# Two plain projections become seven-product pairs, and the scans are packed closer

## The chip, the cores and the metric

The kernel runs on one core of a Trainium2 chip. The metric is the device time of one execution in microseconds (us); the times below are medians over runs, and the profile is one execution taken by the hardware profiler. PE is the matrix engine (TensorE), PEld its weight loads, DVE the vector engine, ACT the scalar engine, POOL GpSimd, SP the engine that issues most DMAs. [...]

## The reference

One layer on 1024 tokens of width 1024, in fp32: two gated feed-forward blocks (width 2816) around a mixer, each behind an RMS norm.

```
h = h + 0.5 * swiglu_ffn(rmsnorm(h, ffn1_norm), ffn1_w_in, ffn1_w_out)
u = rmsnorm(h, mix_norm) @ w_mix_in
cb, cc, ch, gq, gk, gv, gz, gb, ga = split(u)        # 3 x 512, 4 x 512, 4, 4
y_conv = rmsnorm64(cb * causal_conv3(cc * ch)) * conv_out_norm
q, k, v = silu(causal_conv4([gq, gk, gv]))           # 4 heads of 128, q and k normed
beta = sigmoid(gb);  g = -exp(A_log) * softplus(ga + dt_bias)
o = gated_delta_rule_chunked(q, k, v, g, beta)       # a chain of states over chunks
y_gdn = rmsnorm(o, norm_w) * silu(gz)
h = h + concat([y_conv, y_gdn]) @ w_mix_out
h = h + 0.5 * swiglu_ffn(rmsnorm(h, ffn2_norm), ffn2_w_in, ffn2_w_out)
return rmsnorm(h, final_norm)
```

The delta rule solves a triangular system in each chunk and carries a state from chunk to chunk. `cc` is the c gate of the short convolution, `gz` the z gate of the delta rule's output.

## The kernel before, in words

**Products.** Every fp32 operand is split into a high and a low part (`split`, `wsplit`: a cast on ACT, L104, and a subtraction on DVE, L105), and every product is three matmuls (`mm3`, L196 to L200): high x high, low x high, high x low, each 128 x 128 weights against 128 x 512 moving data. Each `mm3` also calls `tick`, a count of groups by which small work is put off with `later(n, f)`.

**Pairs of seven products.** Two column tiles of a weight matrix, the two halves of the contraction and the two halves of the tokens make a 2 x 2 block product, done with seven products instead of eight (class `Pair`, L355 to L485). A product is four `mm3`. The activations' blocks and their sums (A11, A12, S1, nS2, S3, S4, A22) come from class `Blocks`; the weights' sums T1 to T4 are made for each pair on POOL (L112; DVE for the first pairs). `all_pairs` lists the tasks: two pairs run side by side, product by product (`twos`), and the first two products of later pairs (`head1`, `head2`) are put ahead of or between the products of earlier ones. `done` is called with each finished quarter C11, C12, C21, C22.

**Tasks.** A task has a load, a preparation and a run. `run_tasks` runs them in order, with preparations 4 tasks and loads 9 tasks ahead.

**Order.** The code emits instructions in this order; the planner of the framework then lays them on the engines' queues by priority and its own estimate of durations, so a ready `mm3` can be put ahead of a small operation that is not ready. Each engine and each DMA queue works its queue in order.

**Stages.** f1 (first feed-forward) ends near 640 us. The qkv stage (640 to 780 us) runs six pairs over `w_qkv`, in the order n = 4, 6, 0, 2, 8, 10; each finished column tile is stored with its halo (`u_dr`), and the first token half goes through the width-4 convolution (`conv4`, L951) at once, except for n = 10 and 11, whose first halves are stored to `v_dr` and convolved later. In the same stage `project_ba` makes the beta and decay inputs; `gates` (L910) then computes beta and g, in one call of some 30 small DVE operations.

The mixing stage (780 to 1166 us) has these parts:

- `rest`, a generator of plain projections. A unit (`unit_steps`, L1369) is one column tile, two token halves of eight `mm3` each; the generator yields after each `mm3`. There are four z units, then for each of four tiles a c, an h and a b unit: 16 units, 256 `mm3`. A c unit's result is kept in a tile `cc` (L1400), an h unit multiplies it in (L1409) and does the width-3 convolution, a b unit multiplies (L1420) and starts the group norm. `pump(n)` advances `rest` by n `mm3`.
- `late_convs`: 14 convolutions from `v_dr` and `u_dr`.
- `build(c)`, seven steps for each of eight chunks: decay, k k^T, q k^T and scaled copies, stored to DRAM.
- `solve(g)`: inverts 32 x 32 diagonal blocks of four chunks by rows on DVE (L1208, L1212), through DRAM (`diag_l`, `diag_x`).
- `finish(c)` (five steps) assembles a chunk's inverse out of 32- and 64-wide matmuls; `scan(c)` takes the chunk through the state: three links that alternate PE and DVE (L1282, L1287, L1298), the output (L1306, L1307), its norm (L1323, L1327), a transpose and the product with z (L1332), and the store to `y_dr` (L1334).
- `mix_out(part, hf)`: output projection of the convolution part (0) or the delta-rule part (1) for a token half, 32 `mm3` each.

Six chunks are built with 2.7 `mm3` of `rest` at each step (`PACE[0]`). Then scans run in a pipeline in which the next chunk begins after five steps of the last, with 2.05 `mm3` at each scan step and at each step of the last two builds (`PACE[1]`). `scan` forces all z units to be done before chunk 0's output. When chunk 3 is through, the remaining `rest` is emptied, and the order is `mix_out(1, 0)`, `mix_out(0, 0)`, `mix_out(0, 1)`, with two scan steps after each task, then all that is left of the scans, then `mix_out(1, 1)`. f2 (second feed-forward) follows in a new pool scope.

## Time and profile before

| | us |
|---|---|
| median of 3 runs | 1817.4 |
| lowest, highest | 1814.96, 1817.43 |
| profiled execution | 1817.63 |
| its span, first to last instruction | 1815.9 |

| engine | busy us | share |
|---|---|---|
| PE | 1784.8 | 98% |
| PEld | 1456.4 | 80% |
| DVE | 1350.4 | 74% |
| ACT | 738.7 | 41% |
| POOL | 545.5 | 30% |

The mean granted clock of PE is 0.996 of full speed. Busy time is the time in which at least one instruction of the engine was under way; matmuls overlap, so an interval in which PE is 100% busy can still hold more or fewer of them.

In a view of windows a row has the stretch, its length, then for PE, PEld, DVE, ACT and POOL the busy time and the count of instructions, then the granted clock, the DMA engines' share and GB/s. In a view of waits a row has the engine and line that waited, for what, and us in total, number, longest. In a timeline a row has the start, the duration, engine, line, operation, operands; in brackets the idle time before it and what ended it. In a group's row: count, total busy, mean ns of one, idle time before them.

### The profile page before, as it was taken

Reading aid. Unit: us, or ns where it says so; the run is one execution under the profiler, and the core shown is the slowest. Engines: PE = TensorE matmul, PEld = TensorE weight load, DVE = VectorE, ACT = ScalarE, POOL = GpSimd, SP = SyncE. Lnnn points to the kernel's source line nnn. Section 1 sums busy time; section 2 is a strip of 40 time slices with the busy share of each in tenths; the row PEclk is TensorE's granted clock in tenths of the full one; section 3 lists DMA queues with packets and bytes.
Section 4 is the critical chain, followed back from the end, with each engine's and each line's share of the span. In section 5 each row is a group of like instructions: output and inputs, shape, how many; then the busy total and the mean of one; then the engine's idle time right before and its main releaser. Section 6 shows DMA issues by size and latency. Waiting matters only on the chain.

```text
span 1815.9 us, 24900 instructions
## 1 busy us (share of the span) xinstructions
PE 1784.8 (98%) x8476; PEld 1456.4 (80%) x8476; DVE 1350.4 (74%) x2180; ACT 738.7 (41%) x1471; POOL 545.5 (30%) x382
## 2 busy tenths in 40 slices
PE   9999999999999999999999999999999999999997
PEld 6887778888888877778878887788888888888886
DVE  7898877677765889888867666897666666677675
ACT  7532222223534564468342334552222232344443
POOL 0000034446341411302210013016445544435153
PEclk9999999999999999999999999999999999999998
DMA  7435544336974543478854586524433434587542
GB/s 279 161 129 179 175 145 134 128 116 218 335 262 133 167 156 103 147 228 264 258 175 146 154 273 187 173 70 134 158 120 116 150 135 133 167 307 272 199 143 89
DMA packets 198352, 318.75 MB, mean 176 GB/s; under 512 B 28624, under 2 KB 49104, under 8 KB 198224
## 3 DMA queue, kind: packets, MB, share of 16 engines
q1 hardware_dynamic: 195200, 311.85, 51.7%
q10 hardware_dynamic: 3024, 5.30, 0.9%
q8 instruction: 67, 1.10, 0.3%
q14 instruction: 61, 0.50, 0.1%
HBM read 230.54 MB, written 86.53 MB: 175 GB/s over the span
## 4 chain that ended last, share of the span: by engine, by line
PE 43%; DMA 2%; DVE 2%; ACT 1%; issue 1%; POOL 1%; SPq 0%; ACTq 0%; POOLq 0%; DVEq 0%
PE ps_ps L197 12%; PE ps_ps L199 12%; PE ps_ps L198 12%; PE ps_mm L197 2%; PE ps_mm L198 2%; PE ps_mm L199 2%; DMA h<-h_dr 1%; PE ps_aux L1053 1%; DMA raw<-w_mo 1%; PE ps_aux L1079 0%; DVE xb L1212 0%; DVE sv L1208 0%; DVE wlo L105 0%; PE ps_aux L1307 0%; PE ps_aux L1059 0%
## 5 line engine op out<-in xcount | busy, mean ns | idle before, releaser
L197 PE MATMUL ps_ps<-hi,whi 128*128 128x512 f32 x1400 | 547.6, 392 | 5.3 <-DVE c L467 1.9
L199 PE MATMUL ps_ps<-hi,wlo 128*128 128x512 f32 x1400 | 544.8, 390 | 1.2 <-DVE wlo L105 1.1
L198 PE MATMUL ps_ps<-lo,whi 128*128 128x512 f32 x1400 | 545.2, 389 | 0.1
L197 PEld LDWEIGHTS ps_ps<-hi,whi 128*128 128x128 f32 x1400 | 262.8, 188 | 67.9 <-DVE c L467 5.3
L199 PEld LDWEIGHTS ps_ps<-hi,wlo 128*128 128x128 f32 x1400 | 262.8, 188 | 59.5 <-DVE wlo L105 4.9
L112 POOL TENSOR_TENSOR T<-raw 128x512 f32<-128x512 f32 x112 | 173.2, 1547 | 444.9 <-DMA raw<-w_in 230.0
L198 PEld LDWEIGHTS ps_ps<-lo,whi 128*128 128x128 f32 x1400 | 262.9, 188 | 54.5 <-DVE lo L733 0.5
L105 DVE TENSOR_TENSOR wlo<-raw,whi 128x512 fp32r<-128x512 f32 x280 | 239.7, 866 | 74.7 <-ACT whi L104 73.7
L105 DVE TENSOR_TENSOR wlo<-T,whi 128x512 fp32r<-128x512 f32 x244 | 214.4, 890 | 90.3 <-ACT whi L104 87.1
L199 PE MATMUL ps_ps<-ghi,wlo 128*128 128x512 f32 x616 | 241.1, 391 | 0.5 <-DVE wlo L105 0.4
L197 PE MATMUL ps_ps<-ghi,whi 128*128 128x512 f32 x616 | 241.1, 391 | 0.0
L198 PE MATMUL ps_ps<-glo,whi 128*128 128x512 f32 x616 | 240.6, 391 | 0.0
L104 ACT CAST whi<-T 128x512 fp32r<-128x512 f32 x244 | 146.5, 616 | 128.3 <-PE ps_ps L198 44.6
L104 ACT CAST whi<-raw 128x512 fp32r<-128x512 f32 x280 | 169.1, 617 | 60.4 <-DMA raw<-w_out 16.3
L197 PE MATMUL ps_mm<-hi,whi 128*128 128x512 f32 x384 | 157.2, 409 | 1.2 <-DVE u L478 1.2
L105 DVE TENSOR_TENSOR glo<-raw,ghi 128x512 fp32r<-128x512 f32 x154 | 125.0, 811 | 39.9 <-ACT ghi L104 39.2
L198 PE MATMUL ps_mm<-lo,whi 128*128 128x512 f32 x384 | 151.2, 394 | 0.0
L199 PE MATMUL ps_mm<-hi,wlo 128*128 128x512 f32 x384 | 150.8, 393 | 0.0
L199 PEld LDWEIGHTS ps_ps<-ghi,wlo 128*128 128x128 f32 x616 | 115.8, 188 | 26.8 <-DVE wlo L105 1.3
L198 PEld LDWEIGHTS ps_ps<-glo,whi 128*128 128x128 f32 x616 | 115.9, 188 | 25.6
L197 PEld LDWEIGHTS ps_ps<-ghi,whi 128*128 128x128 f32 x616 | 115.8, 188 | 25.3
L104 ACT CAST ghi<-raw 128x512 fp32r<-128x512 f32 x154 | 95.0, 617 | 65.6 <-DMA raw<-f2A 20.0
(254 smaller groups left out, 2144.7 us busy)
## 6 DMA issues: line engine op xcount, KB each, us to landing
raw<-w_in SPq DMA_DIRECT2D x264, 256.0 KB, 4.3
raw<-w_out SPq DMA_DIRECT2D x154, 256.0 KB, 4.2
raw<-w_qkv SPq DMA_DIRECT2D x36, 256.0 KB, 3.3
f1S<-S SPq DMA_DIRECT2D x33, 256.0 KB, 3.8
raw<-f1A SPq DMA_DIRECT2D x33, 256.0 KB, 3.7
raw<-f1S SPq DMA_DIRECT2D x33, 256.0 KB, 3.7
f2S<-S SPq DMA_DIRECT2D x33, 256.0 KB, 4.9
raw<-f2A SPq DMA_DIRECT2D x33, 256.0 KB, 4.4
```

The source lines that it names most:

```text
L104: tc.keep_in_program_order(nc.scalar.copy(out=hi, in_=src))
L105: nc.vector.tensor_tensor(out=lo, in0=src, in1=hi.bitcast(F32), op=ALU.subtract)
L112: tc.keep_in_program_order(nc.gpsimd.tensor_tensor(out=out, in0=in0, in1=in1, op=op))
L197: nc.tensor.matmul(out=ps, lhsT=whi, rhs=xhi, start=start, stop=False, skip_group_check=True)
L198: nc.tensor.matmul(out=ps, lhsT=whi, rhs=xlo, start=False, stop=False, skip_group_check=True)
L199: nc.tensor.matmul(out=ps, lhsT=wlo, rhs=xhi, start=False, stop=stop, skip_group_check=True)
L1053: nc.tensor.matmul(out=ps[:, sl], lhsT=lhs[:, sl], rhs=rhs[:, sl], start=start, stop=stop)
```

## The change

- `all_pairs` gets `heads_at`, which says behind which pair of pairs (`a`) the heads of which later pairs are put; the default is as before.
- The four c units leave `rest` and become two pairs (`c_pair`) at the end of the qkv stage, side by side (`twos` = 0, 2, 4, 6); their heads lie among the products of pairs 2 and 4. Their quarters are stored to `c_dr`, and an h unit loads its `cc` from there when each of its halves begins.
- The convolutions of n = 10 and 11 are done at once, as the others; `v_dr` goes, and `late_convs` has 12 entries.
- `gates` becomes a generator and runs one piece per tick.
- `rest` is now three z units, four times h and b, and the fourth z unit: 12 units, 192 `mm3`. `PACE[1]` is 1.38 instead of 2.05.
- `scan` no longer forces z: the z tile is loaded when `z_done`, and until then the last step is held (`HOLD`); `pipeline` lets the other chunks go on. The rings of `ot` and `zt` tiles get more buffers from rings that the builds used.
- The scan loop ends at `conv_done` instead of chunk 3. The last z unit's `mm3` are spread over six tasks, each followed by scan steps (`go_on`), so that the loads of the output projection, nine tasks ahead, are issued while they run.
- The output projection's order becomes (0, 0), (1, 0), (0, 1), (1, 1), with scan steps after each task. `mix_out(1, hf)` makes sure, when it is prepared, that its chunks are scanned, and loads `y` then.

```diff
-PACE = (2.7, 2.05)
+PACE = (2.7, 1.38)
+LATE_PACE = 1.8
...
-    def all_pairs(pairs, x, norm2, between={}, twos=(0, 2), n_early=EARLY, n_inside=INSIDE):
+    def all_pairs(pairs, x, norm2, between={}, twos=(0, 2), n_early=EARLY, n_inside=INSIDE, heads_at=None):
...
+        if heads_at is None:
+            heads_at = {0: soon}
...
                 if a > 0 or n > 1:
+                    soon = heads_at.get(a, ()) if n == 2 else ()
                     task(*two[0])
-                    for p in soon if a == 0 and n == 2 else ():
+                    for p in soon:
                         task(*p.head1())
                     task(*two[1])
-                    for p in soon if a == 0 and n == 2 else ():
+                    for p in soon:
                         task(*p.head2())
...
+        def by_ticks(steps):
+            if next(steps, steps) is not steps:
+                later(1, lambda: by_ticks(steps))
...
             if hf == 1:
-                gates()
+                by_ticks(gates())
...
             for n in (11, 9, 7, 5, 3, 1):
                 nc.vector.tensor_tensor(out=poly, in0=poly, in1=s2, op=ALU.mult)
                 nc.vector.tensor_scalar(out=poly, in0=poly, scalar1=1.0 / n, scalar2=None, op0=ALU.add)
+                yield
...
-        v_dr = [dram.tile([P, HALF + 3], F32, name=f"v_dr{n}") for n in range(HEADS)]
+        c_dr = [[dram.tile([P, HALF], F32, name=f"c_dr{t}{hf}") for hf in range(NH)] for t in range(4)]
...
-                    if n < 2 * HEADS + 2:
-                        conv4(n + i, 0, t1, temp(F32, "cv"))
-                    else:
-                        nc.sync.dma_start(out=v_dr[n + i - 2 * HEADS], in_=t1[:, 0:HALF + 3])
+                    conv4(n + i, 0, t1, temp(F32, "cv"))
...
-        pairs = [qkv_pair(n) for n in (4, 6, 0, 2, 8, 10)]
+        def c_pair(t):
+            def first(ps):
+                c = temp4(F32, "c11")
+                nc.scalar.copy(out=c[:, 3:HALF + 3], in_=ps)
+                return c
+
+            def done(name, tile_):
+                hf, i = int(name[1]) - 1, int(name[2]) - 1
+                nc.sync.dma_start(out=c_dr[t + i][hf], in_=tile_[:, 3:HALF + 3])
+
+            return Pair(xm, (w_cv[4 + t], w_cv[5 + t]), first, done)
+
+        pairs = [qkv_pair(n) for n in (4, 6, 0, 2, 8, 10)] + [c_pair(t) for t in (0, 2)]
         early_heads(pairs[:EARLY])
-        all_pairs(pairs, xm, nm[1], {0: lambda: project_ba(0), 2: lambda: project_ba(1)}, (0, 2, 4))
+        all_pairs(pairs, xm, nm[1], {0: lambda: project_ba(0), 2: lambda: project_ba(1)}, (0, 2, 4, 6),
+                  n_inside=1, heads_at={2: pairs[6:7], 4: pairs[7:8]})
 
-        order = [w_z[t] for t in range(HEADS)] + [w_cv[i * 4 + t] for t in range(4) for i in (1, 2, 0)]
+        order = [w_z[t] for t in range(3)] + [w_cv[i * 4 + t] for t in range(4) for i in (2, 0)] + [w_z[3]]
...
-            zt = gt_tile("zt", 1)
-            while not z_done:
-                next(rest)
-            nc.sync.dma_start(out=heads(zt), in_=z_dr[hf][:, :, ts])
-            ot = gt_tile("ot", 1)
+            def get_z():
+                zt = gt_tile("zt")
+                nc.sync.dma_start(out=heads(zt), in_=z_dr[hf][:, :, ts])
+                return zt
+
+            yt = get_z() if z_done else None
+            ot = gt_tile("ot")
...
             yield
+            while not z_done:
+                yield HOLD
+            yt = yt or get_z()
             yield
             pyt = flip(ot)
-            yt = zt
-            nc.vector.scalar_tensor_tensor(out=yt, in0=pyt, scalar=vcol(V_GN), in1=zt, op0=ALU.mult, op1=ALU.mult)
+            nc.vector.scalar_tensor_tensor(out=yt, in0=pyt, scalar=vcol(V_GN), in1=yt, op0=ALU.mult, op1=ALU.mult)
...
-                def evac_c(hf, ps):
+                def get_c(hf):
                     cc = mx.tile([P, HALF], F32, name="cc", tag="cs", bufs=3)
-                    nc.scalar.copy(out=cc, in_=ps)
+                    nc.sync.dma_start(out=cc, in_=c_dr[t][hf])
                     ccs.append(cc)
...
-                for evac in (evac_c, evac_h, evac_b):
-                    yield from unit_steps(evac)
+                yield from unit_steps(evac_h, get_c)
+                yield from unit_steps(evac_b)
 
         def others():
-            yield from z_steps()
+            yield from z_steps(range(3))
             yield from conv_steps()
+            conv_done.append(True)
+            yield from z_steps([3])
+            z_done.append(True)
...
-        while CPH - 1 not in scanned:
+        while not conv_done:
             next(scans)
             pump(PACE[1])
             next(side, None)
...
+                if u == 0 and part:
+                    while (hf + 1) * CPH - 1 not in scanned:
+                        advance()
+                    for f in (get, put):
+                        for k in range(4):
+                            f(k)
...
-        def between():
-            for _ in range(2):
-                next(scans, None)
-
-        n_first = len(tasks)
-        task(lambda: [None for _ in rest])
-        mix_out(1, 0, False)
-        run_tasks(n_first + 5, between)
-        mix_out(0, 0, True)
+        steps = [0.0]
+
+        def advance():
+            next(scans, None)
+            next(side, None)
+
+        def go_on(n):
+            steps[0] += n / (LATE_PACE if CPH - 1 in scanned else PACE[1])
+            while steps[0] >= 1:
+                steps[0] -= 1
+                advance()
+
+        def part_of_rest(n):
+            for _ in range(n):
+                next(rest, None)
+                go_on(1)
+
+        for n in (3, 3, 2, 3, 3):
+            task(lambda n=n: part_of_rest(n))
+        task(lambda: [go_on(1) for _ in rest])
+        n_rest = len(tasks)
+        mix_out(0, 0, False)
+        mix_out(1, 0, True)
         task(lambda: norms2[0].after(8, 4))
         norms2[0].then(lambda: [x2.norm1(norms2[0].rb, d) for d in range(KT)])
         mix_out(0, 1, False)
-        run_tasks(len(tasks), between)
-        for _ in scans:
-            pass
-        while queue:
-            tick()
         mix_out(1, 1, True, lambda u: [x2.split1(d) for d in (2 * u, 2 * u + 1)])
...
-        run_tasks(n_mix)
+        run_tasks(n_rest)
+        run_tasks(n_mix, lambda: go_on(4))
```

More of the change, by code (lines that the diff above doesn't have):

```diff
@@ L1364, in conv_norm, with unit_steps @@
             later((16, 10, 10, 7)[t], reduce)
-        z_done = []
-        def unit_steps(evac):
+        z_done, conv_done = [], []
+        def unit_steps(evac, begin=None):
             w = ahead.pop(0)
@@ L1373, in unit_steps @@
             for hf in range(NH):
+                if begin is not None:
+                    begin(hf)
                 ps = psum("mm")
@@ L1381, in unit_steps, with z_steps @@
                 yield
-        def z_steps():
-            for t in range(HEADS):
+        def z_steps(which):
+            for t in which:
                 def evac(hf, ps):
@@ L1391, in z_steps @@
                 yield from unit_steps(evac)
-            z_done.append(True)
         def conv_steps():
@@ L1457, in pipeline @@
                     live.append([gens.pop(0), 0])
+                moved = False
                 for e in list(live):
-                    if next(e[0], live) is live:
+                    said = next(e[0], live)
+                    if said is live:
                         live.remove(e)
-                    else:
+                    elif said is not HOLD:
                         e[1] += 1
+                        moved = True
                         yield
+                if live and not moved:
+                    yield
         scanned = set()
@@ L1521, in tile_hybrid, with mix_out, get, put @@
         norms2 = [Norm(h2[0], "mm"), Norm(h2[1])]
-        def mix_out(part, hf, last, also=None):
+        def mix_out(part, hf, last, also=None, then=None):
             bank = "mm"
-            ys, w = [], {}
+            ys, w = [None] * 4, {}
+            at_once = () if part else range(4 if hf else 3)
+            def get(k):
+                ys[k] = load(y_dr[part][hf][k // 2][:, k % 2, :])
+            def put(k):
+                ys[k] = split(ys[k], slot)
             def loads(u):
                 if u == 0:
-                    ys[:] = [load(y_dr[part][hf][k // 2][:, k % 2, :]) for k in range(4)]
+                    for k in at_once:
+                        get(k)
                 w[u] = [load(w_mo[part, u][:, i * HALF:(i + 1) * HALF]) for i in range(2)]
@@ L1533, in ready @@
                 if u == 0:
-                    ys[:] = [split(y, slot) for y in ys]
+                    for k in at_once:
+                        put(k)
                 w[u] = [wsplit(r) for r in w[u]]
@@ L1539, in ready, with ready_too @@
                         tc.keep_in_program_order(nc.scalar.dma_start(out=h2[hf][d], in_=h_dr[hf][d]))
+                if u == 0 and part:
[4 more added lines that the diff above has]
+                            f(k)
+            def ready_too(u):
+                if u == 0 and len(at_once) == 3:
+                    get(3)
+                    put(3)
+                if also is not None:
+                    also(u)
             def run(u, dd):
```

18 lines of the change are left out of this document (13 added, 5 removed).

## The prediction

> **What bounds the kernel now.** I read the page first (busy shares), then the windows, PE's waits, and the timeline where a wait stood.
>
> ```profile
> span 1815.9 us, 24900 instructions
> PE 1784.8 (98%) x8476; PEld 1456.4 (80%) x8476; DVE 1350.4 (74%) x2180; ACT 738.7 (41%) x1471; POOL 545.5 (30%) x382
> L197 PE MATMUL ps_mm<-hi,whi 128*128 128x512 f32 x384 | 157.2, 409 | 1.2 <-DVE u L478 1.2
> ```
>
> PE is busy 98%, so other engines matter only where they make it wait. The 409 ns of a matmul is its latency; its cost in a stream is the spacing of starts. These windows (us, then busy time and count of PE, weight loads, DVE, ACT, POOL, then the granted clock) give it:
>
> ```profile
> 700.00:750.00 50.00, 49.99 (x220) 37.57 (x219) 46.17 (x66) 23.45 (x46) 14.78 (x13) 1.00 0.39 126
> 750.00:790.00 40.00, 38.36 (x170) 30.64 (x168) 30.64 (x70) 17.53 (x31) 6.29 (x5) 1.00 0.51 163
> 1200.00:1300.00 100.00, 100.00 (x441) 82.40 (x440) 75.71 (x98) 32.46 (x59) 52.23 (x35) 1.00 0.37 120
> ```
>
> 100 us hold 441 matmuls: 0.227 us each. One `mm3` (three matmuls; a "group" below) is 0.68 us. The waits of PE from 640 to 785 us, then from 785 to 1172 us:
>
> ```profile
> PE ps_mm L197 <- DVE u L478: 1.2, 1, 1.2
> PE ps_ps L197 <- DVE poly L935: 0.5, 1, 0.5
> PE ps_ps L199 <- DVE wlo L105: 0.4, 1, 0.4
> ```
> ```profile
> PE ps_aux L1059 <- ACT gd L1327: 1.6, 1, 1.6
> PE ps_ps L197 <- DVE h L1548: 1.5, 1, 1.5
> PE ps_aux L1116 <- DVE gd L1181: 1.3, 1, 1.3
> PE ps_aux L1079 <- DMA xc<-diag_x: 1.2, 1, 1.2
> PE ps_aux L1059 <- DVE xb L1212: 1.0, 1, 1.0
> PE ps_aux L1053 <- DVE gd L1282: 0.8, 2, 0.4
> PE ps_aux L1307 <- DVE gd L1287: 0.5, 1, 0.5
> ```
>
> The largest of them; some 10 us over 530 us, in pieces under 1.7 us. So the stages that the change touches are bound by PE's work, and only some of these waits could also go. None of them is for `w_mo`: the output projection's weights are late for ACT only (3.3 us in four waits below, each from 1030 us on), and PE covers that. Loading them earlier is worth nothing by itself.
>
> ```profile
> ACT whi L104 <- DMA raw<-w_mo: 3.3, 4, 2.3
> ```
>
> **The change part by part.** (1) *The c units as seven-product pairs.* A plain unit is 2 halves x 8 groups x 3 = 48 matmuls, four are 192. A pair does two units in 7 products x 4 groups x 3 = 84 matmuls, two pairs 168. That is 24 fewer: 24 x 0.227 = **-5.4 us** of PE. The mixing stage loses 192 x 0.227 = 43.5 us, the stage before it gains 168 x 0.227 = 38.1 us.
>
> What rides on these 38.1 us, priced by these rows:
>
> ```profile
> L112 POOL TENSOR_TENSOR T<-raw 128x512 f32<-128x512 f32 x112 | 173.2, 1547 | 444.9 <-DMA raw<-w_in 230.0
> L105 DVE TENSOR_TENSOR wlo<-T,whi 128x512 fp32r<-128x512 f32 x244 | 214.4, 890 | 90.3 <-ACT whi L104 87.1
> L104 ACT CAST whi<-T 128x512 fp32r<-128x512 f32 x244 | 146.5, 616 | 128.3 <-PE ps_ps L198 44.6
> L1548 DVE TENSOR_TENSOR h<-ps_mm,h 128x512 f32<-128x512 f32 x32 | 21.9, 687 | 9.8 <-PE ps_mm L199 8.6 <-DMA h<-h_dr 1.1
> L955 DVE SCALAR_TENSOR_TENSOR cv<-u,vs,cv 128x512 f32<-128x512 f32 x42 | 30.7, 763 | 5.3 <-ACT cv L953 5.3
> ```
>
> POOL: 8 weight sums x 1.55 = 12.4 us. ACT: 14 casts x 0.62 = 8.6 us. DVE: 14 splits x 0.89 + 10 additions x 0.69 (priced by the same-shaped L1548) + the two convolutions that no longer go through `v_dr`, 6 x 0.76, = 23.9 us. All lie below 38.1, and the same pattern ran for the pairs ahead of it with the waits shown above, so the cost is 0. If the cover were gone, a late split would cost as there, 0.4 to 0.5 us each; range 0 to +2. The heads of the new pairs go between products of older ones, where 700 to 750 has DVE at 92%: 8 groups x 0.68 = 5.4 us more PE per head against 2 splits, so they relieve DVE.
>
> (2) *Gates one step per group.* The same small DVE operations, spread. They are what the 0.5 us wait on `poly` L935 belongs to: **-0.5**, bounds -0.5 to 0.
>
> (3) *Denser scans.* Counted through the loops: the builds take 42 steps x 2.7 = 113 groups in both kernels. Before, 256 groups of units leave 143 for the scans, plus 96 of the first three `mix_out`: 239. After, 192 leave 79, plus 96: 175 groups for the same 78 scan steps and 14 late build steps. The stretch of before in which 138 groups and 47 scan steps pass, until chunk 3 is scanned and the last unit follows:
>
> ```profile
> 923.00:960.00 37.00, 36.59 (x292) 29.83 (x293) 22.27 (x64) 20.99 (x75) 9.09 (x7) 0.95 0.48 161
> 960.00:1000.00 40.00, 40.00 (x302) 33.28 (x300) 33.53 (x115) 11.38 (x35) 2.74 (x2) 1.00 0.44 133
> 1000.00:1044.00 44.00, 44.00 (x301) 36.63 (x300) 27.00 (x68) 16.72 (x47) 3.65 (x3) 1.00 0.50 151
> ```
>
> DVE worked 82.8 of 121 us (68%). After, up to `z_done`, there are 138 - 79 = 59 groups fewer (40 us), 8 scan steps fewer (priced at one 0.69 us DVE operation and as much PE each, 5.5 us of both) and 3.7 units less to split and evacuate (about five such operations each, 13 us of DVE). That leaves an estimated 64 of 75 us: 86%. DVE does not overtake PE, but a chain has less slack. Each scan step now has 1.38 x 0.68 = 0.94 us of filler instead of 1.39. The waits that belong to scans (L1327 1.6, diag_x 1.2, L1282 0.8, L1287 0.5) sum to 4.1 us; scaled by 239/175 they become 5.6: +1.5. At the other end they shrink, since a chunk's last step is now held back until `z_done`, and the L1327 wait falls out: -1.6. I take **+0.8**, nearer the scaled row. Upper bound +6: the 86% would have to exceed 100% for part of the stretch.
>
> (4) *`c` through DRAM.* Eight 256 KB stores in (1)'s stage, eight loads on SP at the start of a half unit, 8 groups = 5.4 us ahead of L1409. The same-sized loads of `w_cv` land in:
>
> ```profile
> DMA to landing us min/median/max: 3.0/4.2/6.0
> ```
>
> Median 1.2 us early, worst 0.6 late. L1409 waiting would hold the DVE queue behind it (solve, scan); PE has filler. **0**, bounds 0 to 8 x 0.6 = +4.8. The eight 0.6 us ACT copies of `cc` and `v_dr`'s four transfers go; neither stood on PE's path.
>
> (5) *The last z unit held, order of the output projection.* Chunks 0 to 3 write `y` together after `z_done`, 16 groups before `mix_out(1, 0)` is made ready and 32 before it runs: 21.8 us plus some 16 scan steps of PE work. Landing times of `z_dr`, the issue of a `y_dr` store, landing times of `y_dr`:
>
> ```profile
> DMA to landing us min/median/max: 2.8/4.1/7.0
> ```
> ```profile
> L1334 SPq DMA_DIRECT2D y_dr<-gd x16: 525/590/625, 952.5 to 1124.8; - x16
> ...
> DMA to landing us min/median/max: 2.0/3.5/6.4
> ```
>
> They need store and load of z 8.2 + four L1332 3.0 + eight `y_dr` issues 4.7 + store and reload of y 7.0 + cast and split 1.3 = 24.2 us. Covered, by about 10: 0. The end is tighter. Before, chunk 7's last step stands 32 groups ahead of `mix_out(1, 1)`; after, 20. The chain in before:
>
> ```profile
> 1123.43 0.75 DVE L1332 SCALAR_TENSOR_TENSOR gd<-ps_aux,vs,gd 128x512 f32<-128x512 f32 x1 [1.02 <-PE ps_aux L1059]
> ...
> 1130.51 1.37 ACT L104 CAST hi<-raw 128x512 fp32r<-128x512 f32 x2 [5.45 <-DMA raw<-y_dr]
> ```
> ```profile
> 1147.38 0.68 DVE L1548 TENSOR_TENSOR h<-ps_mm,h 128x512 f32<-128x512 f32 x1
> ```
>
> The first `y` is cast 7.1 us after L1332; cast and split make 8.4. The first evacuation of `mix_out(1, 1)` is at 1147.38, so it began 2.7 us earlier, near 1144.5: 21 us of cover, 12 to spare. After, 20 groups and the norm's reduction make about 15 us. But the norm's eight multiplications now fall due at the same group:
>
> ```profile
> L305 DVE SCALAR_TENSOR_TENSOR h<-h,vs,ps_mm 128x512 f32<-128x512 f32 x8 | 5.3, 740 | 0.0
> ```
>
> If all stand before L1332: 8.4 + 5.3 + 0.75 = 14.5, plus the 4 us until chunk 7's `fac` is ready, which partly runs beside them. Wait 0 to +4; I take **+0.5**.
>
> **Sum.** -5.4 - 0.5 + 0.8 + 0 + 0.5 = -4.6. The profiled execution took 1817.6 us (span 1815.9 and 1.7 around it), 0.2 above the median of 1817.4. 1817.6 - 4.6 = 1813.0; stated against the median, **1812.8 us**. About 0.2%, 3.6 us, is what a measurement of this kernel can tell from no change: below 1813.8 counts as faster, above 1821.0 as slower.
>
> **Rivals.** *A, more waits go.* If the L1327 wait (1.6), the diag_x wait (1.2) and the slow clock behind it (1.7, below) vanish with no new ones: -5.4 - 0.5 - 4.5 = -10.4, 1807. For it: all three are single accidents of order. Against it: nothing in the diff touches the solve's round trip through DRAM.
>
> *B, the scans eat the gain.* DVE at 86%, the +6 of (3): 1817.4 - 5.4 - 0.5 + 6 = 1817.5, no change. For it: chains alternate PE and DVE. Against it: PE waited only 0.5 us for L1287 in eight chunks, and 0.8 for L1282.
>
> *C, slower: the clock falls.* One mechanism, at the start of the scans:
>
> ```profile
> 916.00:920.00 4.00, 4.00 (x19) 3.32 (x18) 3.16 (x9) 0.63 (x1) 0.00 (x0) 1.00 0.68 227
> 920.00:923.00 3.00, 1.77 (x8) 1.13 (x6) 0.01 (x1) 0.01 (x1) 0.00 (x0) 1.00 0.37 66
> 923.00:925.60 2.60, 2.59 (x45) 2.06 (x46) 1.86 (x7) 2.48 (x9) 0.00 (x0) 1.00 0.19 30
> 925.60:929.00 3.40, 3.40 (x16) 2.52 (x16) 2.01 (x5) 1.78 (x5) 0.00 (x0) 0.50 0.02 5
> ```
>
> PE waits 1.24 us for diag_x, then runs a burst of 32-wide matmuls, and the next 3.4 us have half the clock: 1.7 us lost. With a third less filler, such stretches come more often. Four more eat the 5.4; six (+10.2) give 1822, slower; eight 1825.5. The 75 us of (3) hold 22 such stretches, so more than one in four would have to fall. Against it: this was the only one in the kernel's middle, though the same scans ran for 200 us. [...]
>
> **How the numbers follow.** Forecast 0.52, A 0.17, B 0.20, C 0.11. The forecast's own range is 1810 to 1815.5, about three quarters of it below 1813.8. Faster 0.39 + 0.17 + 0.02 = 0.58; slower is C with a little of B, 0.11; same 0.31. The range 1806 to 1819.5 holds the forecast, A, and most of B, and leaves out C.
>
> **What would show it.** The count of 128x512 matmuls falls by 24; those in `ps_mm` lose 192. The start of the f2 stage (L1548 of the last group, 1165.9 before) moves as the total does. Step 2: no wait on L935. Step 3: PE's waits on L1282, L1287, L1327, and the granted clock by stretch. Step 4: DVE waiting at L1409 for a DMA. Step 5: PE idle before the first group of `mix_out(1, 1)`. Wrong would be: new waits of more than 4 us in sum, or none of those listed left.

## The result

The changed kernel takes **1843.69 us** (median of 4 runs, 1837.87 to 1847.11); the kernel before took 1817.41 beside it (1814.96 to 1817.81). The ratio is **1.0146, 95% interval 1.0129 to 1.0163**: slower by 26 us, where 4.6 us less were forecast. The profiled execution took 1840.55, with a span of 1838.4.

### The profile page after: what moved, and what is told of

It is laid out like the page before. It is cut to its first block, busy times and chain, and to the rows that moved or that the text cites. A ratio compares the mean times of both kernels' runs of the same rounds, so it can differ in the third digit from the quotient of the medians.

```text
span 1838.4 us, 24917 instructions
## 1 busy us (share of the span) xinstructions
PE 1787.6 (97%) x8452; PEld 1459.1 (79%) x8452; DVE 1360.9 (74%) x2196; ACT 738.1 (40%) x1473; POOL 551.6 (30%) x390
## 4 chain that ended last, share of the span: by engine, by line
PE 43%; DVE 3%; DMA 2%; issue 1%; POOL 1%; SPq 1%; ACT 0%; POOLq 0%; ACTq 0%; DVEq 0%
PE ps_ps L198 11%; PE ps_ps L200 11%; PE ps_ps L199 11%; PE ps_mm L198 2%; PE ps_mm L199 2%; PE ps_mm L200 2%; PE ps_aux L1078 1%; DMA raw<-y_dr 1%; DVE xb L1238 1%; DVE sv L1234 1%; PE ps_aux L1104 0%; DVE wlo L106 0%; PE ps_aux L1332 0%; PE ps_aux L1333 0%; PE ps_aux L1283 0%
## 5 line engine op out<-in xcount | busy, mean ns | idle before, releaser
L198 PE MATMUL ps_ps<-hi,whi 128*128 128x512 f32 x1456 | 569.6, 391 | 5.7 <-DVE c L468 3.5
L200 PE MATMUL ps_ps<-hi,wlo 128*128 128x512 f32 x1456 | 566.3, 390 | 1.8 <-DVE wlo L106 1.8
L199 PE MATMUL ps_ps<-lo,whi 128*128 128x512 f32 x1456 | 566.9, 389 | 0.2 <-DVE lo L737 0.2
L198 PEld LDWEIGHTS ps_ps<-hi,whi 128*128 128x128 f32 x1456 | 273.3, 188 | 70.1 <-DVE c L468 5.8
L200 PEld LDWEIGHTS ps_ps<-hi,wlo 128*128 128x128 f32 x1456 | 273.3, 188 | 61.1 <-DVE wlo L106 4.0
L199 PEld LDWEIGHTS ps_ps<-lo,whi 128*128 128x128 f32 x1456 | 273.4, 188 | 56.6 <-DVE lo L737 0.6
L106 DVE TENSOR_TENSOR wlo<-raw,whi 128x512 fp32r<-128x512 f32 x278 | 233.8, 852 | 74.3 <-ACT whi L105 73.2
L105 ACT CAST whi<-T 128x512 fp32r<-128x512 f32 x252 | 151.2, 616 | 126.9 <-PE ps_ps L199 43.5
L198 PE MATMUL ps_mm<-hi,whi 128*128 128x512 f32 x320 | 133.8, 419 | 7.5 <-ACT hi L105 4.2
L200 PEld LDWEIGHTS ps_ps<-ghi,wlo 128*128 128x128 f32 x616 | 115.8, 188 | 26.7 <-DVE wlo L106 1.3
L199 PE MATMUL ps_mm<-lo,whi 128*128 128x512 f32 x320 | 128.3, 402 | 0.0
L200 PE MATMUL ps_mm<-hi,wlo 128*128 128x512 f32 x320 | 127.3, 398 | 0.0
```

The costliest lines, as they stand in the source:

```text
L105: tc.keep_in_program_order(nc.scalar.copy(out=hi, in_=src))
L106: nc.vector.tensor_tensor(out=lo, in0=src, in1=hi.bitcast(F32), op=ALU.subtract)
L198: nc.tensor.matmul(out=ps, lhsT=whi, rhs=xhi, start=start, stop=False, skip_group_check=True)
L199: nc.tensor.matmul(out=ps, lhsT=whi, rhs=xlo, start=False, stop=False, skip_group_check=True)
L200: nc.tensor.matmul(out=ps, lhsT=wlo, rhs=xhi, start=False, stop=stop, skip_group_check=True)
```

## The profile after

From the page of the changed kernel:

```profile
span 1838.4 us, 24917 instructions
PE 1787.6 (97%) x8452; PEld 1459.1 (79%) x8452; DVE 1360.9 (74%) x2196; ACT 738.1 (40%) x1473; POOL 551.6 (30%) x390
```

PE has 24 instructions fewer, as counted, and is busy 2.8 us longer. Where the time went shows in the first and last start of the plain products, before and after (view of the tile `ps_mm`: count, duration min/median/max, first to last start):

```profile
L197 PE MATMUL ps_mm<-hi,whi x384: 387/389/507, 780.7 to 1164.4; 128*128 128x512 f32 x192
```
```profile
L198 PE MATMUL ps_mm<-hi,whi x320: 387/389/793, 819.0 to 1186.8; 128*128 128x512 f32 x160
```

The mixing stage begins 38.3 us later (38.1 forecast), and lasts 367.8 us instead of 383.7. Its 192 matmuls fewer should have left 383.7 - 43.5 = 340.2. So **27.6 us are lost inside this stage**. From its end to the end of the span both kernels take 651.5 us (1815.9 - 1164.4 and 1838.4 - 1186.8 are 651.5 and 651.6). "Excess" below is this: the length from the first to the last such start, less 383.7 reduced by 0.227 for each matmul moved out.

PE's waits in the stage, after (us in total, times, longest; six rows with 5.0 us lie between the last two shown):

```profile
PE ps_aux L1104 <- DMA xc<-diag_x: 10.7, 1, 10.7
PE ps_mm L198 <- ACT hi L105: 4.2, 2, 3.3
PE ps_mm L198 <- DVE acc L1390: 2.4, 1, 2.4
PE ps_aux L1283 <- ACT junk L1346: 2.4, 1, 2.4
PE ps_aux L1084 <- ACT gd L1355: 1.6, 2, 1.4
PE ps_aux L1145 <- DVE gd L1207: 1.5, 1, 1.5
...
PE ps_aux L1142 <- DVE gd L1207: 0.3, 1, 0.3
```

All rows sum to 28.1 us in 16 waits; the rows of the same view of before sum to 8.9 in 13. That is +19.2. The rest is the clock. Three stretches at half speed (columns as in the prediction's windows: length, busy time and count of PE, PEld, DVE, ACT, POOL, granted clock):

```profile
937.70:944.50 6.80, 6.80 (x23) 5.69 (x22) 5.61 (x18) 3.00 (x5) 3.37 (x2) 0.55 0.97 316
1042.60:1063.10 20.50, 9.85 (x71) 8.24 (x70) 11.32 (x35) 3.95 (x10) 0.00 (x0) 0.51 0.36 109
1087.90:1091.30 3.40, 3.40 (x12) 2.67 (x11) 1.82 (x7) 0.61 (x4) 1.01 (x1) 0.60 0.83 252
```

PE worked 20.05 us in them. Each stretch's busy time times the part of the clock that is missing (6.80 x 0.45 + 9.85 x 0.49 + 3.40 x 0.40) gives 9.2 us lost, against 1.7 before: +7.5. Together that is 26.7 of the 27.6. The longest stretch begins at 1042.6, ahead of the wait for `diag_x`: it stands behind another pause, the 3.3 us (1038.1 to 1041.4) in which PE waits for the cast `hi` of a late `y` tile.

The place of the longest wait, by the timelines of DVE, SP, PE and ACT after (start, duration, engine, line, operation; idle before it and what ended it):

```profile
1041.35 0.69 DVE L106 TENSOR_TENSOR lo<-raw,hi 128x512 fp32r<-128x512 f32 x1 [3.25 <-ACT hi L105]
...
1050.96 0.18 DVE L1238 TENSOR_TENSOR xb<-xb,sv 64x31 f32<-64x31 f32 x1
1051.17 0.48 SPq L1242 DMA_DIRECT2D diag_x<-xb  x1
1055.44 0.60 ACT L1262 COPY x<-xc 32x128 f32<-32x128 f32 x2 [14.13 <-DMA xc<-diag_x]
1055.46 0.87 PE L1104 MATMUL ps_aux<-xc,gd 32*32 32x32 f32 x16 [10.65 <-DMA xc<-diag_x]
1057.31 0.62 ACT L105 CAST whi<-raw 128x512 fp32r<-128x512 f32 x1
```

The rows of the second solve run on DVE until 1050.96; its result goes through DRAM (stored at 1051.17, in use at 1055.44) to chunk 4, the first of the second four. PE, ACT and DVE all have chunk 4's first operation at the head of their queues by then. ACT holds it for 14.1 us, and behind it stand the next casts of `w_mo`, whose loads (issued from 1031.3 to 1042.1, landed within 5.9 us) were there; so PE has no further group of the output projection either. The same place before:

```profile
1011.80 0.48 SPq L1216 DMA_DIRECT2D diag_x<-xb  x1
1016.48 0.59 PE L1079 MATMUL ps_aux<-xc,gd 32*32 32x32 f32 x16
```
```profile
964.00:1012.00 48.00, 48.00 (x350) 40.00 (x349) 41.31 (x140) 13.48 (x41) 5.38 (x4) 1.00 0.40 120
1012.00:1036.00 24.00, 24.00 (x172) 19.71 (x172) 12.67 (x30) 8.73 (x29) 1.01 (x1) 1.00 0.40 114
```

There the round trip took about as long (4.7 us from store to first matmul, 4.3 after), and PE was busy all through it: 16 large matmuls of plain products began in it, and none in the one after. Counted through the loops, 12 groups (8.2 us) stood between the solve's last rows and chunk 4's first step before; after it is one.

## The experiments

The idea under test: 64 groups fewer in the mixing stage leave too few beside the second solve, whose rows are a chain of DVE operations with a DRAM round trip behind it; the queues run up against chunk 4, and PE stands. The expectations split it in two. **S** blames the place: the second solve stands directly ahead of chunk 4, and moving one of them helps. **D** blames the count: the scans have too few groups, wherever the solve stands. A third, **Y**, blames the new order of the output projection, in which a fourth `y` tile is late. In the later texts S says "too few groups beside the second solve's rows", and its rival is the density of the scans or the count. The kernel before had medians of 1815.4 to 1817.8 us beside these runs; ratios are to the runs of the same chip.

| run | median us | ratio, 95% interval | excess us |
|---|---|---|---|
| changed kernel | 1843.69 | 1.0146 [1.0129, 1.0163] | 27.6 |
| e1_hold12 | 1839.16 | 1.0131 [1.0105, 1.0156] | 21.8 |
| e2_pairs_old_order | 1844.88 | 1.0161 [1.0144, 1.0178] | 32.5 |
| e3_order_only | 1825.15 | 1.0051 [1.0036, 1.0066] | 7.4 |
| e4_builds_first | 1827.99 | 1.0066 [1.0049, 1.0083] | 9.3 |
| e5_no_second_rows | 1824.51 | 1.0034 [1.0019, 1.0049] | 12.4 |
| e6_y3_early | 1839.39 | 1.0118 [1.0091, 1.0144] | 28.0 |
| e7_builds_first | 1821.38 | 1.0022 [1.0011, 1.0033] | 5.3 |
| e8_builds_first_pool | 1829.17 | 1.0067 [1.0048, 1.0085] | 14.3 |
| e9_old_order_builds_first | 1828.45 | 1.0064 [1.0046, 1.0081] | 15.6 |
| e10_old_order_builds_first_b | 1830.06 | 1.0069 [1.0054, 1.0084] | 17.7 |
| e11_pace | 1836.07 | 1.0096 [1.0075, 1.0117] | 24.8 |
| e12_warm | 1836.65 | 1.0107 [1.0087, 1.0127] | 25.0 |
| e13_one_pair | 1819.81 | 1.0022 [1.0013, 1.0031] | 1.9 |
| e14_one_pair_b | 1817.59 | 1.0007 [0.9998, 1.0015] | -1.0 |
| e15_one_pair_woven | 1822.25 | 1.0037 [1.0024, 1.0049] | 1.4 |
| e16_one_pair_woven_b | 1829.63 | 1.0075 [1.006, 1.0089] | 7.1 |
| e17_one_pair_kept | 1818.74 | 1.0017 [1.0009, 1.0026] | 3.2 |
| e18_one_pair_woven_kept | 1816.99 | 1.0008 [0.9999, 1.0017] | 1.3 |

The excess is of the one profiled execution, the median of all. Where expectations speak of what PE loses in the mixing stage (28.4 us for the kernel before), they use another count, whose working is not shown; only its differences compare with the excess.

### Which part of the change does it

**e1_hold12**: chunk 4 is held until 12 groups have passed since the second solve's last rows.

```diff
             if c == CPH:
-                for _ in side:
-                    pass
+                while not solved or count[0] < solved[0] + GAP:
+                    yield HOLD
```

> The changed kernel with one edit: chunk 4's finish is held until 12 groups after the second solve is emitted (before had 12 groups between them, the changed kernel has one). Theory S (the solve's round trip): the 10.7 us wait on xc<-diag_x and most of the half clock that follows it go, so 1840 - 10.7 - about 7 = 1822 to 1826. Rival D (scans too dense everywhere): the waits come back at other places, 1835 or more. Rival Y (the late fourth y tile of mix_out(0, 0) starts it all): the 3.3 us wait on the cast of y stays with its half clock, 1828 to 1832.

The median is 4.5 us lower, and the two intervals overlap, so a gain isn't shown. S, with 1822 to 1826, missed; D, with 1835 or more, holds. The wait on `diag_x` went, but others came, the largest:

```profile
PE ps_mm L199 <- ACT hi L106: 3.2, 1, 3.2
PE ps_aux L1105 <- issue: 3.1, 1, 3.1
PE ps_aux L1085 <- ACT gd L1356: 2.8, 2, 1.6
```

Twelve groups put before chunk 4 are missing behind it. The single wait is where the shortage shows, not its amount.

**e2_pairs_old_order**: the kernel before, with the pairs, the spread gates and the direct convolutions, in its own order of the mixing stage.

```diff
-PACE = (2.7, 2.05)
+PACE = (2.7, 1.12)
...
-        order = [w_z[t] for t in range(HEADS)] + [w_cv[i * 4 + t] for t in range(4) for i in (1, 2, 0)]
+        order = [w_z[t] for t in range(HEADS)] + [w_cv[i * 4 + t] for t in range(4) for i in (2, 0)]
```

> The kernel before with the c pairs, the spread gates and the direct convolutions of n = 10, 11, but the old mixing order: z first and forced, mix_out(1, 0) first, two scan steps after each task. The 79 groups left for the scans are spread by a pace of 1.12. Theory S: the pairs' 24 matmuls are saved (-5.4) and nothing stands directly behind the second solve (five scan steps and some six groups between), so 1811 to 1816. Rival D: with even fewer groups per scan step than the changed kernel it is as slow or slower, 1835 to 1845.

```profile
PE ps_aux L1103 <- DMA xc<-diag_x: 13.8, 1, 13.8
```
```profile
1032.70:1053.20 20.50, 8.24 (x71) 7.69 (x72) 10.54 (x35) 4.40 (x15) 0.00 (x0) 0.50 0.15 30
```

The same wait and a half-clock stretch of the same length, without the held z unit and without the new order: S, with 1811 to 1816, missed again, and D holds. The loss needs no new order; it comes with the 64 groups.

**e3_order_only**: the changed kernel's mixing order and densities, c units plain as before.

```diff
-        pairs = [qkv_pair(n) for n in (4, 6, 0, 2, 8, 10)] + [c_pair(t) for t in (0, 2)]
+        pairs = [qkv_pair(n) for n in (4, 6, 0, 2, 8, 10)]
```

> The changed kernel's mixing order and pace (1.38, z unit held, output projection as tasks) with the c gates as plain units as before (256 groups of units, conv_done 64 groups later). Theory S: here more scan steps lie before conv_done, but chunk 4's finish still stands right behind the second solve, so a wait of 5 to 11 us on diag_x with half clock is seen: 1825 to 1840. Rival D (too few groups): there are as many groups as before, so 1815 to 1822.

Here, and in e4_builds_first, more than four chunks are held at their last step, so output tiles are written again before they are used: the values of the delta rule's output change, the work does not. With all 256 groups the order and the densities alone cost 8 us, and PE waits only 0.2 us for `diag_x`. The time lies above D's range and just inside that of S, but the long wait that S asked for isn't there.

**e5_no_second_rows**: the second solve without its row operations.

```diff
-            for j in range(BLK - 1):
+            for j in range(BLK - 1) if g == 0 else ():
```

> The changed kernel, leaving out the row operations of the second solve (some 92 small DVE operations, about 23 us of DVE; its loads and stores stay, so chunks 4 to 7 get no inverse blocks). Theory S (DVE cannot finish the second solve by the time chunk 4 asks for it): the 10.7 us wait and the half clock behind it go, and little comes in their place: 1814 to 1822. Rival D (too few groups for the scans, whatever DVE does): 1832 or more. Rival Y (the fourth y tile): 1828 to 1832, with the 3.3 us wait still there.

The loads and stores of the solve stay; the last four chunks are scanned without their inverse blocks. The `diag_x` wait goes, and 19 of the 26 us with it (1843.69 to 1824.51). That lies between S (1814 to 1822) and D (1832 or more): most of the loss hangs on these rows, not all of it. The largest wait left is this:

```profile
PE ps_aux L1283 <- DVE x L1275: 2.3, 1, 2.3
```

The rows are 25 us of DVE, by the two windows of their lines after:

```profile
1000.00:1051.20 51.20, 12.40 (x46) 0.92 0.58 191
```
```profile
1000.00:1051.20 51.20, 12.52 (x46) 0.92 0.58 191
```

**e6_y3_early**: `mix_out(0, 0)` uses its third `y` tile in the place of the late fourth.

```diff
-                    get(3)
-                    put(3)
+                    ys[3] = ys[2]
```

> The changed kernel with mix_out(0, 0) using its third y tile in place of the fourth, so that nothing in it waits for the last convolution's norm (one load, one cast and one subtraction are left out). Rival Y: the 3.3 us wait on the cast goes, the DVE queue is not held 3.3 us ahead of the second solve's rows, the half clock starts later or not at all: 1826 to 1834. Theory S: the solve is the late one all the same, 1836 to 1842, with a wait on the second diag_x of 7 us or more.

One load, one cast and one subtraction go, and the output has other values. The wait for the cast of `y` fell from 4.2 to 0.9 us, and the `diag_x` wait stayed:

```profile
PE ps_aux L1104 <- DMA xc<-diag_x: 10.5, 1, 10.5
```

The interval overlaps that of the changed kernel. Rival Y falls: the late tile holds up the solve's rows (the 3.25 us of DVE above), but is not what is short.

### More room beside the second solve

**e4_builds_first** and **e7_builds_first**: all eight builds ahead of the scans, so that the second solve can start with them and has all scans of the first four chunks beside it; e7 with 2.35 groups a build step.

```diff
-PACE = (2.7, 1.38)
-LATE_PACE = 1.8
+PACE = (2.35, 1.38)
+LATE_PACE = 1.6
...
-            for _ in pipeline([build(c) for c in (6, 7)], 6):
-                pump(PACE[1])
-                yield
...
-        drive(pipeline([build(c) for c in range(CPH + 2)], 3), PACE[0], side, 1)
+        drive(pipeline([build(c) for c in range(NCH)], 3), PACE[0], side, 1)
```

> The changed kernel with all eight chunks built ahead of the scans (56 steps at 2.0 groups instead of 42 at 2.7, so 112 groups as before), and the second solve beginning with the scans. The second solve then ends some 40 groups ahead of chunk 4's finish. Theory S: no wait on the second diag_x; the build stretch has DVE at about 86% and may wait a few us more: 1815 to 1826. Rival D: the scans are as dense as in the changed kernel, 1835 or more. Rival Y: the 3.3 us wait on y and its half clock stay: 1826 to 1832.

> The changed kernel with all eight chunks built ahead of the scans at 2.35 groups a step (131 groups), the second solve beside the first scans, and a late pace of 1.6. The second solve ends some 20 groups ahead of chunk 4's finish. Theory S: no wait on the second diag_x, PE's lost time in the mixing stage falls to the 28 us of the kernel before plus what the fuller build stretch costs (5 to 10): 1816 to 1824. Rival D: still 175 groups for all scans, 1832 or more.

e4, with 2.0 groups a build step, is 2 us above the range of S; its time lies in that of Y, but it has no wait for the cast of `y`. Its wait on `diag_x` is 0.8 us. e7 lies inside the range of S and takes back 22 of the 26 us with the same pairs and the same 192 groups. Its `diag_x` wait is 0.4 us, its largest waits:

```profile
PE ps_aux L1078 <- DVE gd L1308: 3.2, 3, 1.3
PE ps_mm L1389 <- ACT rw L1386: 2.9, 2, 2.4
```

So in the new order it is largely the place that costs. e7 moves two things away from the scans, the second solve and the last two builds; their shares were not separated. What is left, 5.3 us of excess and 3.2 us behind the mixing stage (654.7 from its last plain product to the end, against 651.5), is more than the 5.4 saved.

**e8_builds_first_pool**: e7 with two 128 x 512 products of each build on POOL.

```diff
-            nc.vector.tensor_tensor(out=kT, in0=kT, in1=eb, op=ALU.mult)
+            nc.gpsimd.tensor_tensor(out=kT, in0=kT, in1=eb, op=ALU.mult)
```

> As e7_builds_first, with the two scaled copies kg and qg of each build multiplied on POOL instead of DVE (16 operations of 0.68 us, 11 us of DVE less, 24 us of POOL more). If DVE is what PE waits for in the build stretch: 3 to 6 us less than e7_builds_first. If PE waits there for chains and transfers, or POOL is in DVE's way: no difference or slower.

8 us slower than e7. PE's longest wait is 8.6 us for ACT's `rw` (L1386). Ahead of it ACT stood 13.0 us at a cast whose load of `w_cv` was late, and SP had issued that load (963.5 us) behind a store of one of POOL's products, for which it waited 3.2 us, and behind stores that wait for DVE. So the edit adds a wait of its own to a queue, and the run doesn't say whether less work on DVE alone would help.

**e9_old_order_builds_first**, **e10_old_order_builds_first_b**: the same in the old order, on e2, with `PACE` (2.0, 1.4) and (2.2, 1.2).

> The kernel before with the c pairs, the spread gates and the direct convolutions, in its own order of the mixing stage, but with all eight builds spread over the front of that stage (2.0 groups a step) and the second solve released only when the scans begin (1.4 groups a step). Theory S (the loss comes from how few groups of matmuls stand beside the second solve's rows, and not from the pairs): no wait on diag_x above 2 us, PE loses some 28 to 35 us in the mixing stage, as in the kernel before (28.4) and in the first build-first run (35.0); with the 5.4 us of matmuls saved that is 1812 to 1819 us. Rival (192 groups of filler are too few wherever the solve stands): 1822 or more, with PE's loss above 38 us, spread over the scans.

> As the run beside it with old order and builds first, but more groups for the builds (2.2 a step) and fewer for the scans (1.2 a step). Theory S: the builds, with the first solve's rows in them, lose less, and the scans begin to lose: within 4 us of the run beside it, 1812 to 1820. Rival (it is the density of the scans that costs): 4 us or more above the run beside it.

A miss for S: 1828 and 1830 instead of 1812 to 1820; the rival of e9 (1822 or more) holds by its time. The `diag_x` wait went, as S has it, but the excess is 15.6 and 17.7. In e9 the largest wait stands at the last build:

```profile
PE ps_mm L197 <- DVE cms L1372: 6.1, 2, 5.9
```

In e10, with more groups there, it moved to the scans, with half-clock stretches of 13.7 and 6.8 us (mean granted clock 0.990, 0.993 in e9). So 192 groups didn't cover builds, solves and scans together in this order in either distribution. Against e2 (32.5) the earlier solve and builds still take back about half.

**e11_pace**: the density undone.

```diff
-PACE = (2.7, 1.38)
+PACE = (2.7, 2.05)
```

> The changed kernel with only the density of its scans undone: 2.05 groups a step once the convolutions' half is reached instead of 1.38. Theory S: the total of groups ahead of the fourth output is what there is, so thinner early scans use it up sooner, and the second solve and chunk 4 fall into fewer groups, not more; no gain, 1838 to 1850, and a wait on diag_x above 8 us. Rival (the density is the cause): 1820 to 1830, and the diag_x wait under 3 us.

The wait on `diag_x` is 7.9 us, the total 1836: 2 us below the range of S and 6 above that of the rival. The 7.6 us against the changed kernel are clear of the noise, but 18 of the 26 stay: density by itself is not the cause.

**e12_warm**: forty matmuls on zeros ahead of chunk 4's first.

```diff
+            if c == CPH:
+                zero = mx.tile([P, HALF], mybir.dt.bfloat16, name="zero")
+                nc.vector.memset(zero, 0.0)
+                warm = psum("aux")
+                for _ in range(40):
+                    tc.keep_in_program_order(
+                        nc.tensor.matmul(out=warm, lhsT=zero[:, 0:P], rhs=zero, start=True, stop=True))
```

> The changed kernel plus forty 128x512 bf16 matmuls on zeros (9 us of PE by 0.227 each) ahead of chunk 4's first matmul, where PE waits 10.7 us for diag_x; nothing reads their result. They add work and take none away. Theory (the wait leaves a half clock behind it that costs half of its 20.5 us, some 10): the wait on diag_x falls to about 2 us, as it is filled with idle work, the half-clock stretch behind it goes, and the total falls by 3 to 10 us, to 1834 to 1841. Rival (the slow clock hides under DVE's chain, which is late anyway): the clock holds at 1.00 and the total stays within 3 us, or rises by up to 9 where the zeros aren't covered.

```profile
1035.80 7.72 PE L1271 MATMUL ps_aux<-zero 128*128 128x512 bf16 x35
1056.94 0.87 PE L1104 MATMUL ps_aux<-xc,gd 32*32 32x32 f32 x16 [4.10 <-DMA xc<-diag_x]
1057.75 2.08 PE L1078 MATMUL ps_aux<-gd 128*128 128x128 f32 x8
```

The view begins in the middle of the zeros, which start at 1034.7. These 9 us of useless matmuls make the kernel 7 us faster. They ran ahead of the wait, not in it, and so left groups for it; the wait fell to 4.1, the half-clock stretch at it to 10.2 (1055.7 to 1065.9, granted clock 0.50). It did not go: eight L1078 still take 2.08 us. What the clock alone costs there was not separated.

### How much can be taken out

**e13_one_pair**, **e14_one_pair_b**: half of part (1), two c units as a pair, two plain, old order; 32 groups fewer, 2.7 us saved.

```diff
-        pairs = [qkv_pair(n) for n in (4, 6, 0, 2, 8, 10)]
+        pairs = [qkv_pair(n) for n in (4, 6, 0, 2, 8, 10)] + [c_pair(0)]
...
-PACE = (2.7, 2.05)
+PACE = (2.7, 1.6)
```

e14 has (2.4, 1.75).

> The kernel before with half of the first part of the change: two of the four c units as one seven-product pair in the stage before (32 groups of matmuls fewer in the mixing stage instead of 64, 12 matmuls or 2.7 us saved), the other two plain; the old order of the mixing stage, 1.6 groups a scan step. Theory 'in proportion' (each group that leaves the mixing stage uncovers about as much of DVE's chain as the last): half of what PE lost more in the run of both pairs in the old order (62.6 - 28.4 = 34.2, so 17.1) against 2.7 saved: 1826 to 1835. Theory 'from a point on' (loss sets in only when the second solve's rows stand directly ahead of chunk 4): its diag_x wait stays under 3 us, PE loses 28 to 33 us, and the total is 1813 to 1820.

> As the run with one pair, with some 13 groups moved from the builds (2.4 a step instead of 2.7) to the scans (1.75 a step instead of 1.6). Theory 'in proportion': it matters little where they stand, within 4 us of the run beside it. Theory 'from a point on': what is short is the groups beside the second solve, so it is as fast or faster, 1812 to 1818.

Both times lie in the ranges of 'from a point on'. The excess is 1.9 and -1.0 us, not the 17 that a loss in proportion asks for: **the first 32 groups cost the mixing stage next to nothing, the second 32 about 30 us** with the same order and six builds ahead of the scans (e2: 32.5; with all builds first 15.6, e9). But the saving isn't there either: the plain products begin at 804.8 and 804.9 instead of 780.7 + 19.1 = 799.8, since the lone pair waits in the stage before (e14):

```profile
793.53 0.75 DVE L1051 SCALAR_TENSOR_TENSOR h<-h,vs,rb 128x512 f32<-128x512 f32 x1 [2.05 <-DMA h<-h_dr]
796.01 0.69 DVE L467 TENSOR_TENSOR c<-ps_ps,p 128x512 f32<-128x512 f32 x1
796.84 0.77 PE L197 MATMUL ps_ps<-hi,whi 128*128 128x512 f32 x1 [2.75 <-DVE c L467]
```

**e15_one_pair_woven**, **e16_one_pair_woven_b**: that pair's products woven between those of the last two qkv pairs; e16 with `PACE` (2.2, 1.9).

```diff
+            for t in (p[0], q[0], p[1], q[1], p[2], pairs[6].head1(), q[2], pairs[6].head2(),
+                      p[3], r[0], q[3], r[1], p[4], r[2], q[4], r[3], r[4]):
+                task(*t)
```

> The second one-pair run with the products of that pair woven between those of the last two qkv pairs, instead of alone behind them. Alone, PE waited 2.8 us for the addition c of L467 and 1.2 us in all for two u of L478, with a half-clock window of 3.4 us behind it: its first ps_mm matmul stood at 804.9 instead of the 780.7 + 19.1 = 799.8 that 84 matmuls cost. If the stage after is long enough for half of the c units (theory 'from a point on'), these 5 us are all that keeps half the change from its own saving of 2.7: 1812 to 1815, first ps_mm at 800 to 801, PE's loss in the mixing stage 28 to 32. Theory 'in proportion': the weave gains 4 to 5 us in the stage before, and the mixing stage gives part of it back: 1815 to 1820.

> As the woven run, with 8 more groups moved from the builds (2.2 a step) to the scans (1.9). If the second solve has groups enough by now, nothing changes: within 2 us of the run beside it; if it is still short, 1 to 3 us faster; if the builds become short (their first solve's rows and the eight norms), 2 to 5 us slower.

Both missed: the wait for L467 stayed (3.4 and 4.5 us), because the scalings of `h` (one of which waits for its load) were still ahead of it in DVE's queue. In e16, with fewer groups at the builds, the excess is 7.1.

**e17_one_pair_kept**, **e18_one_pair_woven_kept**: the scalings put behind L467, with the lone and the woven pair, `PACE` (2.4, 1.75).

```diff
-            nc.vector.scalar_tensor_tensor(out=r, in0=r, scalar=xm.gain(k), in1=rb2, op0=ALU.mult, op1=ALU.mult)
+            tc.keep_in_program_order(
+                nc.vector.scalar_tensor_tensor(out=r, in0=r, scalar=xm.gain(k), in1=rb2, op0=ALU.mult, op1=ALU.mult))
```

> The second one-pair run (pair alone behind the others) with one thing moved: the four scalings of h by rb at the front of the mixing stage stand behind the lone pair's addition c of L467 in DVE's queue, instead of ahead of it, where one of them held the queue 2.05 us for a load of h_dr. If that queue is what makes PE wait 2.8 us for c (and run 3.4 us at half clock after it), the wait falls to about 1 us, the first ps_mm matmul comes at 801 to 803 instead of 804.9, and the total falls by 2 to 4 us: 1813 to 1816. If the scalings are then late for the mixing stage's first group, PE waits there instead and nothing is gained: 1816 to 1819.

> As the run beside it, with the lone pair's products woven between those of the last two qkv pairs. The wait for c of L467 (3.4 us in the first woven run, where the scalings stood ahead of it again) goes altogether, first ps_mm at 800 to 801: 1812 to 1815 if the mixing stage loses 28 to 32 us as in the other one-pair runs; 1816 to 1820 if the scalings are late for the mixing stage.

The wait fell to 1.2 us in e17 and went in e18; the plain products begin at 799.9 and 797.7. In e17 this earlier start gained nothing: the time lies in its second range, and the excess is 3.2. e18 has no half-clock stretch in the middle of its trace (mean granted clock 0.997) and an excess of 1.3, and its profiled execution took 1814.82, but that is the fastest of its eleven. Its median, 1816.99, doesn't differ from before (1815.93 beside it), so what the others lose is not in the trace. e17 is 0.17% slower. No version beat the kernel before.

## Why the prediction was wrong

- **(1), the pairs: right in both counts.** 24 matmuls fewer, the stage before 38.3 us longer against 38.1; what rode along was hidden. PE's waits there after:

```profile
PE ps_ps L198 <- DVE c L468: 1.1, 1, 1.1
PE ps_mm L198 <- DVE u L479: 0.9, 1, 0.9
PE ps_ps L200 <- DVE wlo L106: 0.8, 1, 0.8
```

  They are 2.8 us, against 2.1 in the rows shown of before. What was wrong is the other half of its sentence, "the mixing stage loses 192 x 0.227 = 43.5 us". It lost 15.9.
- **(2), the gates: right.** No wait on the polynomial is left; the 0.5 us can't be seen in the length of that stage.
- **(3), the step that failed.** It took +0.8 us for the fewer groups, at most +6; the mixing stage lost 27.6. It reasoned from averages: DVE's share of a stretch, and the waits of before scaled up by the groups. "DVE does not overtake PE" is true of the stretch, but not of the place. From 1000 to 1030 us DVE is busy 80% of the time and PE 98%, from 1030 to 1051 DVE 76% and PE 54%:

```profile
1000.00:1030.00 30.00, 29.47 (x225) 24.53 (x224) 23.91 (x91) 11.09 (x34) 5.30 (x4) 1.00 0.60 199
1030.00:1051.20 21.20, 11.51 (x48) 8.57 (x46) 16.02 (x42) 3.02 (x6) 0.00 (x0) 0.80 0.56 179
```

  No engine is full there, and PE starves. The wait that grew was not in the list that was scaled: before, PE didn't wait for the second solve's result, because groups covered its round trip. The groups were counted over the stretch (239 and 175); a count that it lacked is the one at this point, from the second solve's last rows to chunk 4's first step (12 and 1). That count alone is not all, as e1 shows: groups put there are missing behind it. The rows of this solve were in the traced stretch, and never priced as a chain: 25 us of DVE, a round trip of 4.3 us, then three queues that hold chunk 4. Leaving the rows out won back 19 us (e5), moving them and two builds earlier 22 (e7).
- **(4), `c` through DRAM: right in size.** PE has no wait for it; DVE waited once, 0.8 us.
- **(5), the order: right at the end, wrong at the front.** Ahead of `mix_out(1, 1)` PE waits 0.9 us (1165.3) for the cast of `y`, where +0.5 stood, and by the mechanism named: all eight multiplications of the norm (L306) stand ahead of chunk 7's product with z (L1362) in DVE's queue:

```profile
1156.59 0.74 DVE L1362 SCALAR_TENSOR_TENSOR gd<-ps_aux,vs,gd 128x512 f32<-128x512 f32 x1
1165.29 0.73 PE L198 MATMUL ps_mm<-hi,whi 128*128 128x512 f32 x2 [0.88 <-ACT hi L105]
```

  The part behind the mixing stage is as long as before. But the fourth `y` tile of `mix_out(0, 0)`, which was not priced, cost PE 3.3 us and DVE 3.25; and order and densities together cost 8 us by themselves (e3), where +0.8 and +0.5 stood.
- **The rivals.** A hoped that the `diag_x` wait of 1.2 us would go, and doubted it because "nothing in the diff touches the solve's round trip through DRAM". That wait was the first solve's (its matmul starts at 923.0 us in the kernel before), and it did go; but the diff took away what covered the round trip of the second solve, and 10.7 us came there, where none had been. C is the nearest: a `diag_x` wait and half clock, and eight windows of 3.4 us for 1825.5; there were nine (30.7 us). But it put them at the start of the scans, one by one, and priced only the clock. By its 1.7 us each, nine would cost 15.3; they cost 9.2, since PE stood idle in much of them anyway. The pauses were the larger part: 19.2 against 7.5.

What stays open: why builds first leave 5.3 us of excess in the new order and 15.6 or 17.7 in the old one; how the loss runs between 32 and 64 groups; what the clock costs by itself; and how much of e7's gain is the solve's and how much the builds'.

## What to carry to other kernels

Matmuls that fill the pauses of a chain aren't free to move: before taking some out of a stage, count what is left between each late producer and its first consumer, place by place, as well as over the stage. Engines that are all below 80% busy can still starve, as here from 1030 to 1051 us, when one operation that waits for a DRAM round trip stands at the head of several queues and the casts for the filler stand behind it. And make such a change by halves: here the mixing stage bore half of it, though no version won the saving, and the other half cost some ten times what it saved.

## What was not expected of the hardware

The granted clock was about half (0.51 and 0.55) behind pauses of 1.5 and 2.75 us, and once stayed there for long although PE worked. In e14_one_pair_b a pause of 2.75 us (above) had this behind it, with large matmuls only:

```profile
797.00:800.40 3.40, 3.40 (x9) 2.68 (x10) 2.75 (x5) 0.61 (x1) 0.00 (x0) 0.55 0.20 77
```

In e5_no_second_rows, at the start of the scans, 13.7 us ran at half clock with PE busy all of them, on small matmuls for the most part, behind a pause of 1.5 us that ended at 975.3. Before, during and after:

```profile
960.00:977.40 17.40, 15.86 (x156) 12.20 (x154) 11.63 (x33) 12.66 (x47) 3.77 (x3) 0.99 0.56 182
977.40:991.10 13.70, 13.70 (x73) 11.73 (x73) 5.21 (x18) 3.90 (x15) 3.08 (x2) 0.51 0.31 100
991.10:1005.00 13.90, 13.90 (x120) 11.68 (x118) 9.32 (x26) 3.46 (x16) 2.60 (x2) 1.00 0.58 189
```

The same wait of the changed kernel (L1145 for `gd`, 1.5 us, ended at 977.0) had the full clock behind it, 1.00 until 985.0, and so had the 1.65 us of the kernel before that ended at 1122.3 (1.00 until 1130.0). From what pause on the clock falls, and after how much work it returns, these runs don't show.
